# Values in an attention block: high and low half in one stationary tile, summed in DRAM

## The chip, the cores and the metric

The kernel runs on one core of one Trainium2 chip. The metric is device microseconds of one execution on that core, taken as the median of several runs of the same program. Times inside a run come from one profiled execution, as microseconds from its first instruction. PE is the matmul engine (PEld its weight load), DVE the vector engine, ACT the scalar engine, POOL is GpSimd, and SP issues most DMAs.

## The reference

One decoder block for S = 1024 positions and a model width of 1024, in float32. The part that matters here, cut down:

```
proj = rmsnorm(x) @ w_in + b_in
u_pool, q, k, v, gates = split(proj)          # 512, 512, 128, 128, 2048 columns
# pooling: four groups of 128 channels, windows 2, 4, 8, 16
y_pool = ((window_mean(u) - u) @ w_pool) * pool_scale
# attention: 8 query heads of 64, 2 key/value heads, blocks of 128 queries, window 128
p = softmax([s * 0.125 + mask, sink])[..., :-1]
o = einsum('bnhgqk,bnkhd->bnqhgd', p, v)      # y_attn
merged = sigmoid(g_pool) * (y_pool @ w_branch_pool) + sigmoid(g_attn) * (y_attn @ w_branch_attn)
x = x + rmsnorm(merged @ w_out)
x = x + rmsnorm(relu(rmsnorm(x) @ w_up)**2 @ w_down)
```

## The kernel before

**Halves.** Every float32 operand of a matmul is split into a high float32r part (a cast, `split` L99, by ACT) and a low part (the value minus the high part, L104, by DVE). A product is then three matmuls: high by high, low by high, high by low. All matmuls accumulate in PSUM banks of 128x512.

**Stages.** The program goes through the projections (to about 81 us), the attention loop (81 to 182), the gate products (to 334), the attention and pooling branches with their merge (334 to about 420), the output projection and the MLP. In the first two stages the order of work on PE, DVE and ACT is the order of the code. POOL's and SP's orders, and all orders in the branch stage, are set by the framework's scheduler.

**The attention loop** (L767 to L810) has one turn n for each of the eight blocks of 128 queries. A turn transposes the probabilities of block n (`attend_t`, L376; two head groups kv, one bank "at" each, split by ACT and DVE into four tiles), issues the scores of block n+2 (`score`, L333), forms the masked copy of the probabilities (`attend_own`, L385), transposes q and k of block n+3 into two "at" banks and splits them (`post_qkv`, L294; tiles `qt`, `khi`, `klo`), runs softmax pieces (maximum on DVE, L349 to L351; exponentials on ACT, L357 and L359; the scale on DVE, L363 to L365), and ends with the product of probabilities and values (`attend_v`, L394). Three banks carry the name "at", three "mm". Between these pieces `fill(t)` takes about t microseconds of PE work from a generator `others()`: the projections of the remaining blocks, then for each pooling group `u_half` (L575, u of one half of the positions) and `wb_half` (L594, the pooling weights folded into the branch weights). Half way through each `u_half` the list `between[th]` is flushed: weight splits and copies for later (casts `wh` and L561 on ACT, low halves L104 and L562 on DVE).

**The value product.** `attend_v(n)` for n > 0 has two terms: all probabilities by the values of block n−1, and the masked ones by the difference of the values of blocks n and n−1 (`dv`). A stationary tile holds, for high and low, the columns [head 0, zeros, head 1]: a slice of 128 columns from 0 or from 64 puts one head into its own half of the output rows and zeros into the other. So both head groups accumulate in one bank, with 3 × 2 matmuls a term. POOL makes these tiles (`split_v`, L281 writes the zeros). Two ACT copies of 128x256 (L398) move the bank into `y` tiles, which live in SBUF until four blocks are done and are then stored to DRAM in four transfers of 512 KB.

**Pooling sums.** `pool_in` (L655 to L665) adds the bias and builds windowed sums by doubling steps on DVE: one step for window 2, four for window 16. For groups 2 and 3 `pump` runs single steps inside turns 4 to 7 of the loop, before u goes to DRAM. For groups 0 and 1 the raw u goes to DRAM, and `pool_part` sums it in the branch stage.

**The branch stage.** Eight attention branches (`branch`, L422 and L424 on PE) each fill two banks "mm" of four and end with two gate products on DVE (L918). `pool_part` follows branches 2, 3, 5 and 6: it loads one group of u (L923, tile `d`), sums it where needed, and splits it. `load_attn` brings `y` back from DRAM ahead of the stage.

Of the kernel before, what the change touches and what calls it, by code (L numbers as in the profile page):

```python
# [8 lines left out]
F32 = mybir.dt.float32  # L9
F32R = mybir.dt.float32r  # L10
# [4 lines left out]
P = 128  # L15
# [33 lines left out]

@with_exitstack  # L50
def block_kernel(ctx: ExitStack, tc, xt, x, consts, vecs, sinks, b_qkv, g_post, g_mlp, g_mlp_post,
                 w_qkv, w_u, w_g, w_pool, w_bp, w_ba, w_o, w_up, w_dn, x1_dram, spill, wbp_dram, f_dram, out):
    nc = tc.nc
    act, dve, pool, pe = nc.scalar, nc.vector, nc.gpsimd, nc.tensor

# [9 lines left out]
    z_dram, y_dram, u_dram = (spill[i:j] for i, j in ((0, 16), (16, 20), (20, 24)))  # L65
    cnt = [0]

    def nm(s):
        cnt[0] += 1
        return f"{s}_{cnt[0]}"  # L70
# [25 lines left out]
    def f32(ap):  # L96
        return ap.bitcast(F32)
# [150 lines left out]
    khi = at("khi", 1, [S], F32R)  # L248
    klo = at("klo", 1, [S], F32R)
    vs, dvs = {}, {}  # L250
    y = [[None, None], [None, None]]
    for th in range(2):
        for kh in range(2):
            y[th][kh] = yy.tile([P, 2, 512], F32, tag="y", name=nm("y"))
    qts = {}

    tfs = {}

    def pre_qkv(n):
        tf = y[1][n - 2].rearrange("p a b -> p (a b)") if n in (2, 3) else at("qkv", 3, [1024])  # L260
# [126 lines left out]

    def attend_v(n):
        pt, pc = probs.pop(n)
        yb = bank("at", [4, P])  # L390
        mms = [(v, p, kv, j) for v, p in (((vs[n - 1], pt), (dvs[n], pc)) if n else ((vs[0], pt),))
               for j in ((0, 0), (1, 0), (0, 1)) for kv in range(2)]
        for j, (v, p, kv, (vh, ph)) in enumerate(mms):
            pe.matmul(yb.rearrange("p m q -> p (m q)"), v[:, vh, kv * HD:kv * HD + P],  # L394
                      p[ph][:, 4 * kv:4 * kv + 4].rearrange("p i q -> p (i q)"), start=j == 0, stop=j == len(mms) - 1)
        c = (n % 4) * P
        for g in range(2):
            act.copy(y[n // 4][g][:, :, c:c + P], yb[:, 2 * g:2 * g + 2])  # L398


    rb = bcp.tile([P, 1024], F32, tag="bc", name="rb_all")
# [163 lines left out]
    def u_half(gi, th):  # L565

        if th == 0:
            ut[gi] = ga_.tile([P, S], F32, tag="ga", name=nm("u"))
        (whi, wlo), u = wu[gi], ut[gi]
        sl = slice(th * 512, (th + 1) * 512)  # L570
        b = bank("mm")

        mms = [(k, xh, 0) for k in range(NK) for xh in range(2)] + [(k, 0, 1) for k in range(NK)]
        for j, (k, xh, h) in enumerate(mms):
            pe.matmul(b, (whi, wlo)[h][:, k, :], xr(k, xh, th), start=j == 0, stop=j == len(mms) - 1)  # L575
            if j == 7:
# [4 lines left out]
        if th == 1 and gi < 2:  # L581
            nc.sync.dma_start(u_dram[gi], u)
        elif th == 1:
            us[gi] = u

    def wb_half(gi, dj):

# [13 lines left out]
                                  t.rearrange("c (m n) -> c m n", n=P))  # L601
        between[dj].append(out)

    us, ut, wt, wpts = {}, {}, {}, []

    def others():
        for n in range(4, NT):
# [114 lines left out]
    with tc.manual_schedule(engines={mybir.EngineType.PE, mybir.EngineType.DVE, mybir.EngineType.Activation}):  # L722
        for n in range(NT):
            fill(0.34)
            pe.matmul(bss[:, n:n + 1], sq[:, n * P:(n + 1) * P], ones, start=n == 0, stop=n == NT - 1)
        rsqrt(r1, bss[:, :NT], NT)
        act.activation(warm, r1[:, :1], AF.Exp)
        pre_qkv(0)
        pre_qkv(1)
        fill(5.4)  # L730
        post_qkv(0)
        pre_qkv(2)
        fill(2.8)
# [24 lines left out]
        sums = {}  # L758

        def pump(k, gi):  # L760

            if gi not in sums:
                sums[gi] = pool_in(gi, us[gi], y_place)
            for _ in range(k):
                next(sums[gi])

        for n in range(NT):  # L767
            attend_t(n)
            if n == 0:
                softmax_exp(1, LOW)  # L770
            if n + 2 < NT:
                score(n + 2, 0)
            if n + 1 < NT:
                softmax_exp(n + 1, HIGH)
            if n + 2 < NT:
                score_prev(n + 2, 0)
            attend_own(n)
# [16 lines left out]
            if n == 4:  # L794
                pump(1, 3)
            elif n == 5:
                pump(2, 3)
                nc.sync.dma_start(u_dram[3], us.pop(3))
            elif n == 6:
                pump(2, 2)  # L800
                load_x(0, lambda: at("qkv", 3, [S]))
            elif n == 7:
                pump(1, 2)
                nc.sync.dma_start(u_dram[2], us.pop(2))
                gt.prepare(0)
            fill(3.0 if n == NT - 1 else 4.2)
            attend_v(n)
            if n % 4 == 3:
                for kh in range(2):
# [73 lines left out]
    def load_attn():  # L883
        for kh in range(2):
            for th in range(2):
                ws = stage([2, 512])
                nc.sync.dma_start(flat(ws), y_dram[2 * th + kh])
# [565 lines left out]
```

## Time and profile before

| | us |
|---|---|
| runs, median (lowest to highest of 3) | 1137.67 (1136.68 to 1137.91) |
| span of the profiled execution | 1136.2 |
| ACT's copy of one value bank, 2 x 128x256 (L398), a pair | 0.65 |
| DVE's low half of a weight, 128x1024 (L104) | 1.22 |
| gate product in the branch stage (L918), a pair | 1.28 |
| PE busy, in the windows from 80 to 182 us | 102.00 of 102.00 |

The profiled execution is one run with the span from its first to its last instruction; a run's device time has about 1.5 us around that. In the rows of the timeline the first number is the start, the second the duration; a note in brackets tells how long the engine stood still before, and which engine ended that. In the rows of groups the mean of one instruction is in nanoseconds.

### The profile page before, as it was taken

The numbers are of one execution on the slowest core, as the hardware profiler recorded it, in microseconds if no ns is written. First come the engines' busy times: TensorE is split into PE (matmuls) and PEld (weight loads), VectorE is DVE, ScalarE is ACT, GpSimd is POOL, SyncE is SP. The second block draws the span as 40 slices with busy tenths as digits, with TensorE's granted clock in tenths as the row PEclk, the third lists the DMA queues.
The fourth block names the chain that finished last, engine by engine and source line by source line (L and its number), as shares of the span: only waits on it lengthen the run. The fifth ranks groups of instructions, "written<-read, shape, count | busy, mean of one in ns | idle before, by whom it ended". The sixth has DMA issues, their size and how long they took to land.

```text
span 1136.2 us, 14006 instructions
## 1 busy us (share of the span) xinstructions
PE 1120.7 (99%) x5213; PEld 926.6 (82%) x5213; DVE 822.7 (72%) x1210; ACT 523.9 (46%) x912; POOL 65.3 (6%) x110
## 2 busy tenths in 40 slices
PE   8999999999999999999999999999999999999997
PEld 7888888888888888888788888888888888888885
DVE  7668797899956685677998666666457955446887
ACT  6346655454522234455655444444444345344352
POOL 3432100000000230000000000000000000000000
PEclk9999999999999999999999999999999999999999
DMA  7202338356664434333265343434687765332652
GB/s 247 84 1 74 116 108 297 129 188 229 217 234 161 139 142 155 112 145 111 108 236 206 139 164 142 160 146 156 223 321 278 244 198 193 109 93 74 219 191 91
DMA packets 72052, 186.94 MB, mean 165 GB/s; under 512 B 6448, under 2 KB 10672, under 8 KB 71984
## 3 DMA queue, kind: packets, MB, share of 16 engines
q1 hardware_dynamic: 66368, 166.38, 42.0%
q10 hardware_dynamic: 5616, 19.66, 4.5%
q8 instruction: 41, 0.67, 0.2%
q14 instruction: 27, 0.22, 0.1%
HBM read 132.54 MB, written 53.48 MB: 164 GB/s over the span
## 4 chain that ended last, share of the span: by engine, by line
PE 91%; DVE 5%; ACT 2%; DMA 2%; issue 1%; DVEq 0%
PE mm L485 22%; PE at L485 15%; PE at L1291 14%; PE mm L1291 11%; PE mm L1008 6%; PE mm L422 5%; PE mm L575 4%; PE mm L183 3%; PE mm L424 3%; PE at L394 2%; PE sc L333 1%; PE at L1008 1%; PE at L192 1%; DVE wh L104 1%; DMA st<-in_w_up_dram 1%
## 5 line engine op out<-in xcount | busy, mean ns | idle before, releaser
L1291 PE MATMUL at<-ar,wh 128*128 128x512 f32 x744 | 169.6, 389 | 0.0
L1291 PEld LDWEIGHTS at<-ar,wh 128*128 128x128 f32 x744 | 139.6, 188 | 29.3 <-DVE ar L104 0.4
L1291 PE MATMUL mm<-ar,wh 128*128 128x512 f32 x576 | 131.0, 389 | 0.0
L104 DVE TENSOR_TENSOR wh<-raw,wh 128x1024 fp32r<-128x1024 f32 x53 | 64.8, 1223 | 85.4 <-ACT wh L101 85.4
L1291 PEld LDWEIGHTS mm<-ar,wh 128*128 128x128 f32 x576 | 108.1, 188 | 22.5
L101 ACT CAST wh<-raw 128x1024 fp32r<-128x1024 f32 x53 | 55.8, 1053 | 135.8 <-PE at L1291 61.9
L101 ACT CAST wh<-st 128x512 fp32r<-128x512 f32 (+1 forms) x105 | 66.2, 642 | 104.0 <-PE at L485 31.0
L104 DVE TENSOR_TENSOR wh<-st,wh 128x512 fp32r<-128x512 f32 (+1 forms) x105 | 81.8, 790 | 25.9 <-ACT wh L101 23.3
L485 PE MATMUL mm<-gr,wh 128*128 128x512 f32 x309 | 74.5, 390 | 0.1
L485 PEld LDWEIGHTS mm<-gr,wh 128*128 128x128 f32 x309 | 57.7, 188 | 12.3 <-ACT g L1073 0.5
L485 PE MATMUL mm<-T,wx 128*128 128x512 f32 x288 | 67.6, 389 | 0.0
L485 PEld LDWEIGHTS mm<-T,wx 128*128 128x128 f32 x288 | 54.1, 188 | 11.2
L485 PE MATMUL at<-T,wx 128*128 128x512 f32 x252 | 59.1, 389 | 0.0
L485 PEld LDWEIGHTS at<-T,wx 128*128 128x128 f32 x252 | 47.3, 188 | 9.8
L485 PE MATMUL mm<-x,wh 128*128 128x512 f32 x240 | 55.2, 389 | 0.0
L485 PEld LDWEIGHTS mm<-x,wh 128*128 128x128 f32 x240 | 45.0, 188 | 9.4
L104 DVE TENSOR_TENSOR ar<-B,ar 128x1024 fp32r<-128x1024 f32 x37 | 45.1, 1219 | 5.3 <-ACT ar L101 5.0
L575 PE MATMUL mm<-x,wh 128*128 128x512 f32 x192 | 47.5, 396 | 0.0
L485 PE MATMUL at<-gr,wh 128*128 128x512 f32 x174 | 42.4, 390 | 0.0
L101 ACT CAST ar<-B 128x1024 fp32r<-128x1024 f32 x37 | 38.9, 1050 | 7.5 <-DMA B<-in_w_dn_dram 4.7
L575 PEld LDWEIGHTS mm<-x,wh 128*128 128x128 f32 x192 | 35.2, 188 | 7.7
L485 PEld LDWEIGHTS at<-gr,wh 128*128 128x128 f32 x174 | 32.6, 188 | 7.3 <-DVE gr L104 0.5
(368 smaller groups left out, 2182.9 us busy)
## 6 DMA issues: line engine op xcount, KB each, us to landing
raw<-f_dram SPq DMA_DIRECT2D x53, 512.0 KB, 3.7
f_dram<-g SPq DMA_DIRECT2D x30, 512.0 KB, 3.3
B<-in_w_dn_dram SPq DMA_DIRECT2D x24, 512.0 KB, 6.2
st<-in_w_up_dram SPq DMA_DIRECT2D x22, 512.0 KB, 3.5
st<-in_w_g_dram SPq DMA_DIRECT2D x18, 512.0 KB, 3.6
f_dram<-g ACTq DMA_DIRECT2D x17, 512.0 KB, 2.6
g<-spill_dram SPq DMA_DIRECT2D x16, 512.0 KB, 4.5
raw<-in_w_dn_dram SPq DMA_DIRECT2D x16, 512.0 KB, 4.6
```

The costliest lines, as they stand in the source:

```text
L101: act.copy(hi, src)
L104: eng.tensor_tensor(lo, src, f32(hi), ALU.subtract)
L183: pe.matmul(bq, xs_[k][n // 4][:, xh, n % 4 * P:(n % 4 + 1) * P], wq[k][:, h, :], start=k == 0 and j == 0, stop=k == NK - 1 and j == 2)
L192: pe.matmul(bkv_of(n), xs_[k][n // 4][:, xh, n % 4 * P:(n % 4 + 1) * P], wkv[k // 2][:, h, k % 2, :], start=k == 0 and j == 0 and not (joi ...
L333: pe.matmul(sb[:, kv, i, :nk], qt[r, qx, m * P:(m + 1) * P], kx[r, k0:k0 + nk], start=j == 0, stop=j == 2)
L394: pe.matmul(yb.rearrange("p m q -> p (m q)"), v[:, vh, kv * HD:kv * HD + P], p[ph][:, 4 * kv:4 * kv + 4].rearrange("p i q -> p (i q)"), st ...
L422: pe.matmul(bs[th], whi[:, k, :], rhs(k, hl, th), start=k == 0 and hl == 0, stop=False)
L424: pe.matmul(bs[th], wlo[:, k, :], rhs(k, 0, th), start=False, stop=k == nk - 1)
L485: pe.matmul(b, w[:, wh, kt, :], xo[kt][:, xh, :], start=not after and kt == 0 and j == 0, stop=kt == 3 and j == 2, skip_group_check=after)
L575: pe.matmul(b, (whi, wlo)[h][:, k, :], xr(k, xh, th), start=j == 0, stop=j == len(mms) - 1)
L1008: pe.matmul(obs[n][dj], l, wos[k][whl][:, dj * 512:(dj + 1) * 512], start=k == 0 and hl == 0 and whl == 0, stop=k == NK - 1 and hl == 1)
L1291: pe.matmul(bs[t], fo[fh][:, k2, t * P:(t + 1) * P], wo_[wh][:, k2, :], start=not after and s2 == 0 and k2 == 0 and j == 0, stop=s2 == NS ...
```

## The change

- **One stationary tile for both halves.** `split_v` now makes tiles with the columns [high, low] of one head, without zeros. One matmul with the high part of p then gives high by high in output rows 0 to 63 and low by high in rows 64 to 127; a second one, with the low part of p, adds the rest. A term needs two matmuls for each head group. Each head group has its own bank, and the loop's `bank("at")` is called twice.
- **The halves are added in DRAM.** ACT copies each bank whole into a tile `yt` (a fresh one for each turn, from a pool of four). SP writes rows 0 to 63 into `y_dram`, in two transfers of 128 KB; POOL then adds rows 64 to 127 in two accumulating transfers of the same size. `y_dram` has a new layout, and `load_attn` reads it so.
- **Held flushes.** While the `fill` right ahead of `attend_v` runs, `u_half` does not flush `between[th]`; that is done after `attend_v`.
- **Later pooling sums.** `pump` is gone. All four groups store their raw u, and `pool_part` sums each.

The core of the diff:

```
     def split_v(src, tag, bufs):
-        t = at(tag, bufs, [2, 3, HD], F32R)
-        pool.memset(f32(t[:, :, 1, :]), 0.0)
-        split(t[:, 0, ::2, :], t[:, 1, ::2, :], src, pool, pool)
-        return t.rearrange("p l a d -> p l (a d)")
+        t = at(tag, bufs, [2, 2, HD], F32R)
+        split(t[:, :, 0, :], t[:, :, 1, :], src, pool, pool)
+        return t.rearrange("p a l d -> p a (l d)")
...
     def attend_v(n):
         pt, pc = probs.pop(n)
-        yb = bank("at", [4, P])
-        mms = [(v, p, kv, j) for v, p in (((vs[n - 1], pt), (dvs[n], pc)) if n else ((vs[0], pt),))
-               for j in ((0, 0), (1, 0), (0, 1)) for kv in range(2)]
-        for j, (v, p, kv, (vh, ph)) in enumerate(mms):
-            pe.matmul(yb.rearrange("p m q -> p (m q)"), v[:, vh, kv * HD:kv * HD + P],
-                      p[ph][:, 4 * kv:4 * kv + 4].rearrange("p i q -> p (i q)"), start=j == 0, stop=j == len(mms) - 1)
-        c = (n % 4) * P
-        for g in range(2):
-            act.copy(y[n // 4][g][:, :, c:c + P], yb[:, 2 * g:2 * g + 2])
+        yt = yy.tile([P, 2, 4, P], F32, tag="y", name=nm("yt"))
+        terms = ((vs[n - 1], pt), (dvs[n], pc)) if n else ((vs[0], pt),)
+        rows = y_dram[n // 4][:, :, n % 4 * P:(n % 4 + 1) * P]
+        for kv in range(2):
+            yb = bank("at", [4, P])
+            mms = [(v, p) for v, pp in terms for p in pp]
+            for j, (v, p) in enumerate(mms):
+                pe.matmul(flat(yb), v[:, kv, :], flat(p[:, 4 * kv:4 * kv + 4]), start=j == 0, stop=j == len(mms) - 1)
+            act.copy(yt[:, kv], yb)
+        for kv in range(2):
+            nc.sync.dma_start(rows[kv * HD:(kv + 1) * HD], yt[:HD, kv])
+        for kv in range(2):
+            pool.dma_start(rows[kv * HD:(kv + 1) * HD], yt[HD:, kv], accum_op=ALU.add)
...
     # u_half
             if j == 7:
-                flush(between[th])
+                if held[0]:
+                    held.append(th)
+                else:
+                    flush(between[th])
...
     # the loop
-            if n in (4, 5):
-                pump(1, 3)
-            elif n == 6:
-                pump(1, 2)
             fill(3.6)
...
+            held[0] = True
             fill(3.0 if n == NT - 1 else 4.2)
             attend_v(n)
-            if n % 4 == 3:
-                for kh in range(2):
-                    nc.sync.dma_start(y_dram[n // 4 * 2 + kh], flat(y[n // 4][kh]))
+            held[0] = False
+            while len(held) > 1:
+                flush(between[held.pop()])
...
     def pool_part(gi):
         u = yy.tile([P, S], F32, tag="y", name=nm("d"))
         nc.sync.dma_start(u, u_dram[gi])
-        if gi < 2:
-            for _ in pool_in(gi, u, y_place):
-                pass
+        for _ in pool_in(gi, u, y_place):
+            pass
```

Three places in the order of the engines. On PE, at the end of turn 3 (`s_190` to `s_197` are the split probabilities, `at_1444` the value bank, `at_1463` and `at_1470` the banks of the transposes of turn 4), before:

```order
L594 MATMUL mm_1440<-wh_1133,wpt 128x512
L394 MATMUL at_1444<-s_190_1301,v_741 128x512 x4
L394 MATMUL at_1444<-s_191_1302,v_741 128x512 x2
L394 MATMUL at_1444<-s_196_1337,dv_915 128x512 [waits DVE_49]
L394 MATMUL at_1444<-s_196_1337,dv_915 128x512 x3
L394 MATMUL at_1444<-s_197_1338,dv_915 128x512 [waits DVE_49]
L394 MATMUL at_1444<-s_197_1338,dv_915 128x512
L376 MATMUL at_1463<-cst,s_171_1167 128x128 [waits DVE_49]
L376 MATMUL at_1463<-cst,s_171_1167 128x128 x3
L376 MATMUL at_1470<-cst,s_171_1167 128x128 [waits DVE_49]
L376 MATMUL at_1470<-cst,s_171_1167 128x128 x3
```

The same place now (`at_1439` and `at_1445` are the two value banks, `at_1457` and `at_1464` those of the transposes):

```order
L392 MATMUL at_1439<-s_194_1296,v_736 128x512
L392 MATMUL at_1439<-s_195_1297,v_736 128x512
L392 MATMUL at_1439<-s_200_1332,dv_907 128x512 [waits DVE_49]
L392 MATMUL at_1439<-s_201_1333,dv_907 128x512 [waits DVE_49]
L392 MATMUL at_1445<-s_194_1296,v_736 128x512 [waits DVE_49]
L392 MATMUL at_1445<-s_195_1297,v_736 128x512
L392 MATMUL at_1445<-s_200_1332,dv_907 128x512
L392 MATMUL at_1445<-s_201_1333,dv_907 128x512
L371 MATMUL at_1457<-cst,s_173_1162 128x128 [waits DVE_49]
L371 MATMUL at_1457<-cst,s_173_1162 128x128 x3
L371 MATMUL at_1464<-cst,s_173_1162 128x128 [waits Activation_49]
L371 MATMUL at_1464<-cst,s_173_1162 128x128 x3
```

The wait for DVE that stood at the first transposes (the bank that held the transposed q, until DVE has its low half) stands at the second value bank, and the second group of transposes waits for ACT, for the copy of the first value bank.

On ACT, at the end of turn 2 (`es` and `s_171` or `s_173` are the exponentials, `wh` a weight of the filler work, `s_190` or `s_194` the probabilities of turn 3), before:

```order
L357 ACTIVATE es_1226<-es_1226 128x8
L359 ACTIVATE s_171_1167,den_1227<-s_171_1167,nmx_1225 128x128 x4
L101 CAST wh_1270<-st_1118 128x1024
L398 COPY y_459<-at_1286 128x2x128
L398 COPY y_460<-at_1286 128x2x128
L101 CAST s_190_1301<-at_1303 128x512
L101 CAST s_190_1301<-at_1310 128x512
```

And now:

```order
L352 ACTIVATE es_1221<-es_1221 128x8
L354 ACTIVATE s_173_1162,den_1222<-s_173_1162,nmx_1220 128x128 x4
L393 COPY yt_1275<-at_1276 128x512
L393 COPY yt_1275<-at_1282 128x512
L101 CAST wh_1292<-st_1111 128x1024
L101 CAST s_194_1296<-at_1298 128x512
L101 CAST s_194_1296<-at_1305 128x512
```

The weight's cast has gone behind the value copies, and stands right ahead of the casts of the next turn's probabilities.

On DVE, in the branch stage around the gate products of branches 3 to 5 (`g` the gate, `mm` the bank, `d` and `t` the pooling sums), before:

```order
L104 TENSOR_TENSOR yplo_3412<-d_3409,yphi_3411 128x1024
L104 TENSOR_TENSOR yplo_3454<-d_3451,yphi_3453 128x1024
L918 TENSOR_TENSOR g_3288<-g_3288,mm_3296 128x512
L918 TENSOR_TENSOR g_3288<-g_3288,mm_3297 128x512
L104 TENSOR_TENSOR wh_3420<-st_3417,wh_3419 128x512
L918 TENSOR_TENSOR g_3337<-g_3337,mm_3345 128x512
L918 TENSOR_TENSOR g_3337<-g_3337,mm_3346 128x512
```

And now:

```order
L898 TENSOR_TENSOR g_3256<-g_3256,mm_3264 128x512
L898 TENSOR_TENSOR g_3256<-g_3256,mm_3265 128x512
L660 COPY t_3386<-t_3383 128x4
L663 SCALAR_TENSOR_TENSOR d_3377<-t_3386,d_3377 128x1017
L664 TENSOR_TENSOR t_3386<-t_3386,cst 128x7
L104 TENSOR_TENSOR wh_3401<-st_3398,wh_3400 128x512
L665 TENSOR_TENSOR d_3377<-t_3386,d_3377 128x7
L659 TENSOR_TENSOR t_3435<-d_3432 128x1023
L104 TENSOR_TENSOR yplo_3393<-d_3377,yphi_3392 128x1024
L898 TENSOR_TENSOR g_3305<-g_3305,mm_3313 128x512
L898 TENSOR_TENSOR g_3305<-g_3305,mm_3314 128x512
```

The sums of groups 2 and 3 stand between the gate products; the first step of the last group (`d_3432`) stands ahead of branch 4's.

More of the change, by code (lines that the diff above doesn't have):

```diff
@@ L51, in block_kernel @@
 def block_kernel(ctx: ExitStack, tc, xt, x, consts, vecs, sinks, b_qkv, g_post, g_mlp, g_mlp_post,
-                 w_qkv, w_u, w_g, w_pool, w_bp, w_ba, w_o, w_up, w_dn, x1_dram, spill, wbp_dram, f_dram, out):
+                 w_qkv, w_u, w_g, w_pool, w_bp, w_ba, w_o, w_up, w_dn, x1_dram, spill, y_dram, wbp_dram, f_dram, out):
     nc = tc.nc
@@ L63, in block_kernel @@
     psum = {"pool": psa_pool.__enter__(), "bufs": {"sc": 1, "at": 3, "mm": 3}}
-    z_dram, y_dram, u_dram = (spill[i:j] for i, j in ((0, 16), (16, 20), (20, 24)))
+    z_dram, u_dram = (spill[i:j] for i, j in ((0, 16), (16, 20)))
     cnt = [0]
@@ L250, in block_kernel @@
     vs, dvs = {}, {}
-    y = [[None, None], [None, None]]
-    for th in range(2):
-        for kh in range(2):
-            y[th][kh] = yy.tile([P, 2, 512], F32, tag="y", name=nm("y"))
     qts = {}
@@ L259, in pre_qkv @@
     def pre_qkv(n):
-        tf = y[1][n - 2].rearrange("p a b -> p (a b)") if n in (2, 3) else at("qkv", 3, [1024])
+        tf = yy.tile([P, 1024], F32, tag="y", name=nm("y")) if n in (2, 3) else at("qkv", 3, [1024])
         tfs[n] = tf
@@ L580, in u_half @@
         dve.tensor_tensor(u[:, sl], b, rb[:, sl], ALU.mult)
-        if th == 1 and gi < 2:
+        if th == 1:
             nc.sync.dma_start(u_dram[gi], u)
-        elif th == 1:
-            us[gi] = u
     def wb_half(gi, dj):
@@ L602, in wb_half @@
         between[dj].append(out)
-    us, ut, wt, wpts = {}, {}, {}, []
+    ut, wt, wpts, held = {}, {}, [], [False]
     def others():
@@ L757, in block_kernel @@
         fill(3.7)
[L758 to L765, printed above, removed]
         for n in range(NT):
@@ L793, in block_kernel @@
                 softmax_exp(n + 2, LOW)
[L794 to L800, printed above, removed]
+            if n == 6:
                 load_x(0, lambda: at("qkv", 3, [S]))
             elif n == 7:
-                pump(1, 2)
-                nc.sync.dma_start(u_dram[2], us.pop(2))
                 gt.prepare(0)
+            held[0] = True
             fill(3.0 if n == NT - 1 else 4.2)
             attend_v(n)
-            if n % 4 == 3:
-                for kh in range(2):
-                    nc.sync.dma_start(y_dram[n // 4 * 2 + kh], flat(y[n // 4][kh]))
+            held[0] = False
+            while len(held) > 1:
+                flush(between[held.pop()])
         gt.prepare(1)
@@ L886, in load_attn @@
                 ws = stage([2, 512])
-                nc.sync.dma_start(flat(ws), y_dram[2 * th + kh])
+                nc.sync.dma_start(ws, y_dram[th][:, 2 * kh:2 * kh + 2])
                 hi = xp.tile([P, 2, 512], F32R, tag="x", name=nm("yahi"))
@@ L1444 @@
     x1 = nc.dram_tensor("x1_dram", (NT, P, D), F32, kind="Internal").ap()
-    spill = nc.dram_tensor("spill_dram", (24, P, S), F32, kind="Internal").ap()
+    spill = nc.dram_tensor("spill_dram", (20, P, S), F32, kind="Internal").ap()
+    yd = nc.dram_tensor("y_dram", (2, P, 4, 512), F32, kind="Internal").ap()
     wbp = nc.dram_tensor("wbp_dram", (8, P, 4, P), F32, kind="Internal").ap()
@@ L1449 @@
     with tile.TileContext(nc) as tc:
-        block_kernel(tc, *args, x1, spill, wbp, fd, out)
+        block_kernel(tc, *args, x1, spill, yd, wbp, fd, out)
     r = run_bass_kernel_spmd(nc, [arrays], core_ids=[0])
```

## The prediction

> **What bounds the kernel now.** I read the busy times on the page and the chain that ended last first, then the busy time by windows around the two places that the change touches: the attention loop (87 to 182 us) and the branch stage (from 334 us).
>
> ```profile
> span 1136.2 us, 14006 instructions
> PE 1120.7 (99%) x5213; PEld 926.6 (82%) x5213; DVE 822.7 (72%) x1210; ACT 523.9 (46%) x912; POOL 65.3 (6%) x110
> ...
> PE 91%; DVE 5%; ACT 2%; DMA 2%; issue 1%; DVEq 0%
> ```
>
> PE is busy for 99% of the span and is 91% of the chain. The windows (stretch, sum, then PE, PEld, DVE, ACT, POOL with their counts, granted clock, DMA share, GB/s) show the same in the stages concerned:
>
> ```profile
> 80.00:100.00 20.00, 20.00 (x144) 17.45 (x143) 16.14 (x28) 11.23 (x41) 1.95 (x6) 1.00 0.08 27
> 100.00:120.00 20.00, 20.00 (x122) 16.28 (x121) 15.94 (x23) 13.10 (x43) 8.88 (x19) 1.00 0.31 106
> 120.00:140.00 20.00, 20.00 (x120) 16.14 (x119) 16.92 (x26) 13.07 (x39) 2.26 (x7) 1.00 0.38 128
> 140.00:160.00 20.00, 20.00 (x112) 16.27 (x111) 19.04 (x32) 10.65 (x37) 2.01 (x6) 1.00 0.17 57
> 340.00:360.00 20.00, 20.00 (x90) 16.57 (x89) 15.26 (x24) 7.09 (x9) 0.00 (x0) 1.00 0.68 230
> 360.00:380.00 20.00, 20.00 (x90) 16.57 (x89) 7.69 (x13) 3.44 (x5) 0.00 (x0) 1.00 0.18 56
> ```
>
> PE has no gap in any of them, at full clock: a matmul that goes shortens the span, as long as nothing that PE needs comes late instead. The follower is DVE: 19.04 of 20 us in the late loop, 7.69 of 20 at 360. So work taken from DVE in the loop is relief, and work put at 360 has room.
>
> **The matmuls that go.** These are the value product's matmuls, and its place in the third full turn of the loop (n=3):
>
> ```profile
> L394 PE MATMUL at<-s,v x48: 389/389/393, 87.1 to 178.8; 128*128 128x512 f32 x48
> L394 PE MATMUL at<-s,dv x42: 389/389/393, 100.9 to 180.2; 128*128 128x512 f32 x42
> ```
> ```profile
> 128.19 1.52 PE L394 MATMUL at<-s,v 128*128 128x512 f32 x6
> 129.55 1.53 PE L394 MATMUL at<-s,dv 128*128 128x512 f32 x6
> 130.91 1.03 PE L376 MATMUL at<-cst,s 128*128 128x128 f32 x8
> ```
>
> Twelve matmuls take 130.91 − 128.19 = 2.72 us, so one costs 0.227 us (389 ns is its latency; they are pipelined). Of 48 + 42 = 90, n=0 keeps 4 of 6 and the other seven turns 8 of 12: 60 stay, 30 go. 30 × 0.227 = **6.8 us**: 0.45 in n=0 and 0.91 in each later turn. The new matmuls have the same shape, so I give them the same 0.227.
>
> **The waits that come.** Two things now stand close behind one another. First, the second value bank of a turn is the one that the q transposes of post_qkv(n+3) just used, so its first matmul waits for DVE's low half of q. Before, that wait lay 2.72 us behind the start of the value matmuls, at the transposes; now 0.91 us. Second, the second head group's transposes of attend_t(n+1) wait until ACT has copied the first value bank. ACT in n=2 and n=3, and DVE between:
>
> ```profile
> 112.47 0.21 ACT L357 ACTIVATE es<-es 128x8 f32<-128x8 f32 x1 [2.14 <-DVE es L351]
> ...
> 114.13 1.03 ACT L101 CAST wh<-st 128x1024 fp32r<-128x1024 f32 x1
> 117.00 0.65 ACT L398 COPY y<-at 128x256 f32<-128x256 f32 x2 [1.84 <-PE at L394]
> 117.53 1.10 ACT L101 CAST s<-at 128x512 fp32r<-128x512 f32 x2
> ...
> 128.08 0.21 ACT L357 ACTIVATE es<-es 128x8 f32<-128x8 f32 x1 [3.41 <-DVE es L351]
> ...
> 129.65 0.19 ACT L359 ACTIVATION_READ_ACCUMULATOR s<-s,nmx 128x1 f32 x1
> ```
> ```profile
> 99.03 0.68 DVE L104 TENSOR_TENSOR qt<-at,qt 128x512 fp32r<-128x512 f32 x1
> ...
> 112.36 0.68 DVE L104 TENSOR_TENSOR qt<-at,qt 128x512 fp32r<-128x512 f32 x1
> ...
> 115.19 1.22 DVE L104 TENSOR_TENSOR wh<-st,wh 128x1024 fp32r<-128x1024 f32 x1 [1.36 <-ACT wh L101]
> 118.17 1.29 DVE L104 TENSOR_TENSOR s<-at,s 128x512 fp32r<-128x512 f32 x2 [1.75 <-ACT s L101]
> ...
> 127.96 0.69 DVE L104 TENSOR_TENSOR qt<-at,qt 128x512 fp32r<-128x512 f32 x1
> ```
> ```profile
> 99.51 1.52 PE L394 MATMUL at<-s,v 128*128 128x512 f32 x6
> ...
> 114.07 1.52 PE L394 MATMUL at<-s,v 128*128 128x512 f32 x6
> ```
> ```profile
> L335 ACT COPY s<-sc 128x512 f32<-128x512 f32 x11 | 6.5, 588 | 8.6 <-PE sc L333 8.3
> ```
>
> *Turn n=2.* With 0.45 + 0.91 won, its value matmuls start at 112.7. The copies now have the shape of L335, 0.59 us. The first bank is full 0.91 later, at 113.6; the exponentials (1.78 us from es at 112.47, by n=3's 129.84 − 128.08 = 1.76) end at 114.2 if they don't come earlier, so the copy ends at 114.8. PE would want the bank after eight matmuls and four transposes, 1.82 + 0.5 after the start, at 115.0. I take **0.2** us.
>
> *Turn n=3* is the dearest. The held flush puts the cast of wh (1.03) and DVE's low half of it (1.22) behind both copies: copies to about 115.3, cast to 116.3, low half to 117.5. DVE begins its two splits of s then, against 118.17 before: 0.67 us earlier. From there to the low half of q, DVE has no pause in the trace, so that ends at 128.65 − 0.67 = 128.0. PE has won 0.45 + 0.91 + 0.91 − 0.2 = 2.1 by then: value matmuls from 126.1, second bank wanted at 127.0. It waits 1.0. The exponentials also come 0.67 earlier, ending at 129.2, the first copy at 129.8; PE would be at the second transposes 1.4 after 128.0, at 129.4: 0.4 more. **1.4 us** in this turn.
>
> *Turn n=4* has no held weight in front of it (the copies are followed by the casts of s directly), so DVE follows PE closer; I take half, **0.7**. *Turn n=5* has no q transposes left, only the copy behind the exponentials; DVE loses a pooling sum ahead of them. I take **0.3**. Turns 6 and 7 have no exponentials. At n=1 the low half of q ends at 99.71, and the second bank is wanted at 99.51 − 0.45 + 0.91 = 99.97; at n=2 the two are 113.04 and 113.6: room, though little at n=1.
>
> Sum: 0.2 + 1.4 + 0.7 + 0.3 = **2.6 us** come back as waits; both ends for the range are 0 (all inside the slack) and 6.8 (four turns at n=3's price, 5.6, and more behind).
>
> **What moves beside PE.** The longer copies add 2 × 0.48 − 0.65 = 0.3 us a turn to ACT (11 to 13 of 20 busy), counted above. The memsets leave POOL. Pooling sums leave the loop:
>
> ```profile
> L659 DVE TENSOR_TENSOR t<-t 128x1022 f32<-128x1022 f32 (+2 forms) x5 | 6.1, 1213 | 0.0
> ...
> L659 DVE TENSOR_TENSOR t<-u 128x1023 f32<-128x1023 f32 x2 | 2.4, 1217 | 0.0
> L663 DVE SCALAR_TENSOR_TENSOR u<-t,u 128x1009 f32<-128x1009 f32 (+1 forms) x2 | 2.4, 1210 | 0.0
> L655 ACT ACTIVATE u<-u,vec 128x1024 f32<-128x1024 f32 x2 | 2.3, 1150 | 0.0
> ```
>
> That is 6.1 + 2.4 + 2.4 = 10.9 us on DVE, some 12 with the short pieces. They turn up between the gate products of the branch stage:
>
> ```profile
> 361.65 1.29 DVE L918 TENSOR_TENSOR g<-g,mm 128x512 f32<-128x512 f32 x2 [3.55 <-PE mm L424]
> ```
> ```profile
> 334.47 0.39 PE L422 MATMUL mm<-yahi,wh 128*128 128x512 f32 x1
> ...
> 339.91 0.39 PE L422 MATMUL mm<-yahi,wh 128*128 128x512 f32 x1
> ```
> ```profile
> DMA to landing us min/median/max: 4.3/6.3/7.6
> ```
>
> A branch takes PE 339.91 − 334.47 = 5.44 us; with four banks, two a branch, the gate product of branch m must be done when branch m+2 starts, at 334.47 + 5.44 (m+2): 5.44 us of room. DVE idles 3.55 us a branch from 361 on. Twelve us over four branches is 3 each: it fits, barely. The two loads of u stand ahead: DVE's first sum of the last group waits for a load that can only start when a buffer is free, by my count at about 358 in the old clock. Landing in 4.5 us, plus 1.15 (L655), 1.2 (L659) and 0.7 for the first half of the gate product, ends at 365.6; branch 6 wants that bank at 367.1. Landing in 6.3 costs 0.3; in 7.6 it costs 1.6 there, and about 2 with the next branches. At 360 to 380 the DMA share is 0.18 against 0.68 before, so I take the short landing, **0**.
>
> **The DMAs.** Four stores of 512 KB become sixteen of 128 KB on SP and sixteen that add, on POOL. No accumulating transfer is in the trace. The nearest rows of issue, SP's, are 0.33 us each, and a turn has two. What stands behind them on POOL is the split of the next V:
>
> ```profile
> 145.99 0.46 POOL L104 TENSOR_TENSOR dv<-df,dv 128x128 fp32r<-128x128 f32 x1
> ...
> 177.67 1.52 PE L394 MATMUL at<-s,v 128*128 128x512 f32 x6
> ```
>
> The last V is ready at 146.5 and used at 179: over 30 us to spare. From the first store at about 91 to 177 POOL has 86 us, less the 15 that it is busy in the four windows from 80 to 160: 71 us for the eight transfers ahead of the last V, so PE stalls only from about 9 us each. Bounds: 0, and all that lies above that; I take 0, by the 0.33.
>
> **Sum.** 6.8 − 2.6 = 4.2 us off the profiled 1136.2: 1132.0. The runs' median is 1137.67, 1.5 above that span, so **1133.5**.
>
> **The rivals.**
> *All of it arrives:* DVE, relieved of its sums, and the exponentials come earlier by as much as PE. For it: DVE idles in the early loop (15.94 of 20). Against: the 10 us without a pause before 127.96. The time is 1137.7 − 6.8 = 1130.9. Chance 0.17.
>
> *The loop closes on itself:* each of turns 1 to 4 waits as n=3 does, 4 × 1.4, and n=5 adds 0.3: 5.9 of 6.8 are gone, 1136.8; with the loads landing in 7.6 us, 1138.8. Here belongs, too, that the change doesn't shorten PE at all. For it: PE's turn is 14.1 − 0.9 = 13.2 us, and the round from the second bank over copy, cast, DVE's low half and the 10.5 us to q is 0.9 + 0.6 + 1.0 + 1.2 + 10.5 = 14.2. Against: only one turn has a full wh held. Chance 0.22.
>
> *Slower:* the last pooling sums sit ahead of the gate products on DVE, and each branch from m=4 on waits for loads. It decides against the change when the wait passes 4.2 + 2.3 = 6.5 us, which by the sum above needs a landing of 6.0 + 6.5 = 12.5 us; at 15.2, twice the worst row, the wait is 9.2 and the time 1142.7. Against: the three landings quoted. Chance 0.06.
>
> *Slower by POOL:* if an accumulating transfer holds POOL for 12 us, eight cost 96, 25 more than the 71 us: 1158. DVE is busy 19.04 of 20 us at 140, so a transfer that POOL could issue only while DVE rests would take 20 times 0.33, 6.6 us: short of the 9. Chance 0.04. The Trainium skill ("DMA: Bandwidth & Descriptors", section SWDGE vs HWDGE vs iDMA) states such a lock: transfers that accumulate come from GpSimd alone, and the descriptor rings that it writes for them lie in the SBUF state that a two-port mode of DVE keeps it out of. No run here shows it; by that rule an issue would stretch towards the 6.6.
>
> **How the numbers follow.** 4.2 less, give or take 1.2: chance 0.51, all of it faster by more than 0.2% (2.3 us), about the least that a measurement of this kernel tells from no change. With the full gain, 0.17: faster 0.68; of the closed loop nearly all is within 0.2%: same 0.21; slower 0.11. The range goes from 1130.5 (the full gain) to 1138.5 (the closed loop with late loads).
>
> **What would show it.** L392's matmuls should be 60 at 0.227 us. PE should show waits at L392's second bank on DVE (qt), longest at n=3, and at L371 on ACT (yt), in sum 1 to 4 us. DVE's busy time falls in 140 to 182 and rises in 350 to 380. If PE waits at L422 for DVE's L898, the loads were late; if at L392 for POOL, the transfers. A loop that is shorter by 6.8 us makes me wrong in the waits, a PE gap after 182 in the rest.

## The result, and the profile after

| | before | after |
|---|---|---|
| runs, median (lowest to highest of 5) | 1137.91 (1136.68 to 1139.01) | 1133.95 (1132.40 to 1134.51) |
| ratio of after to before, 95% interval | | 0.9963 (0.9951 to 0.9975) |
| span of the profiled execution | 1136.2 | 1132.7 |
| first value matmul of n=0 to the end of the last of n=7 | 93.30 | 89.03 |

The change makes the kernel faster, by 4.0 us in the medians; forecast were 4.2, with 1133.5. (A run's device time lies 1.7 to 1.8 us above its own span, 1134.51 and 1132.7 here; the 1.5 given ahead is the median of the runs before less the span of one of them.) The page of after, its first lines and its chain:

```profile
span 1132.7 us, 14023 instructions
PE 1114.8 (98%) x5183; PEld 920.9 (81%) x5183; DVE 820.6 (72%) x1210; ACT 526.7 (47%) x912; POOL 77.8 (7%) x111
...
PE 87%; DVE 7%; ACT 3%; DMA 2%; issue 1%; SPq 0%; DVEq 0%; ACTq 0%
```

PE has 30 instructions less (5213 to 5183) and is busy 5.9 us less, yet the span fell by 3.5 only, and DVE and ACT have taken shares of the chain. The windows of after (stretch, sum, busy time of PE, PEld, DVE, ACT, POOL, clock, DMA share, GB/s) show where:

```profile
120.00:140.00 20.00, 19.01 (x114) 14.86 (x113) 17.88 (x25) 11.26 (x32) 4.95 (x8) 1.00 0.74 168
140.00:160.00 20.00, 19.26 (x107) 15.39 (x107) 12.88 (x22) 13.19 (x41) 3.48 (x6) 1.00 0.49 113
160.00:180.00 20.00, 20.00 (x94) 16.63 (x93) 13.77 (x19) 10.37 (x25) 4.04 (x4) 1.00 0.81 198
360.00:380.00 20.00, 20.00 (x90) 16.58 (x89) 15.13 (x26) 4.52 (x8) 0.00 (x0) 1.00 0.26 79
```

PE has gaps now in two windows of the loop, 1.0 and 0.7 us, and none at 360 to 380, where DVE went from 7.69 to 15.13 us busy. The gaps in PE's timeline of after (start, duration; in brackets the pause ahead and who ended it):

```profile
126.51 0.62 PE L392 MATMUL at<-s,v 128*128 128x512 f32 x2
126.96 0.61 PE L392 MATMUL at<-s,dv 128*128 128x512 f32 x2
128.54 0.73 PE L392 MATMUL at<-s,v 128*128 128x512 f32 x2 [0.97 <-DVE qt L104]
129.12 0.62 PE L392 MATMUL at<-s,dv 128*128 128x512 f32 x2
129.57 1.28 PE L371 MATMUL at<-cst,s 128*128 128x128 f32 x8
...
148.75 0.39 PE L328 MATMUL sc<-klo,qt 64*128 64x256 f32 x2 [0.16 <-DVE s L337]
...
155.95 0.60 PE L371 MATMUL at<-cst,s 128*128 128x128 f32 x4
157.12 0.66 PE L371 MATMUL at<-cst,s 128*128 128x128 f32 x4 [0.57 <-ACT yt L393]
```

At n=3 the second bank would have started four matmuls after the first, at 127.42; it starts 1.12 late, and DVE's low half of q ends that wait. At n=5 the second transposes come 0.7 late, behind ACT's copy of the first bank. (A bracket counts from the modelled end of the last matmul, so it shows a little less than the start times do.)

Counted by turns, from the first value matmul of one to that of the next:

| turn | before | forecast without waits | after | waits |
|---|---|---|---|---|
| 0 to 1 | 12.42 | 11.97 | 11.98 | 0.0 |
| 1 to 2 | 14.56 | 13.65 | 13.65 | 0.0 |
| 2 to 3 | 14.12 | 13.21 | 13.21 | 0.0 |
| 3 to 4 | 14.34 | 13.43 | 14.89 | 1.46 |
| 4 to 5 | 13.40 | 12.49 | 12.73 | 0.24 |
| 5 to 6 | 11.55 | 10.64 | 11.45 | 0.81 |
| 6 to 7 and the last product | 12.91 | 11.10 | 11.12 | 0.0 |

The waits are 2.5 us in all, and 93.30 − 6.8 + 2.5 = 89.0. The first value matmul itself starts 0.58 later (87.09 and 87.67), and what follows the last one takes 956.0 against 955.8: −4.27 + 0.58 + 0.2 = −3.5, the difference of the spans. The 0.58 arises in the first stage: behind a pause of PE at 53 us the matmuls resume at 55.52 in before and 56.17 in after, and at 55.18 to 55.90 in the other traces, most of which have the same order up to there. So it is taken as scatter, not as an effect of the change.

### The profile page after: what moved, and what is told of

It is laid out like the page before. It is cut to its first block, busy times and chain, and to the rows that moved or that the text cites. A ratio compares the mean times of both kernels' runs of the same rounds, so it can differ in the third digit from the quotient of the medians.

```text
span 1132.7 us, 14023 instructions
## 1 busy us (share of the span) xinstructions
PE 1114.8 (98%) x5183; PEld 920.9 (81%) x5183; DVE 820.6 (72%) x1210; ACT 526.7 (47%) x912; POOL 77.8 (7%) x111
## 4 chain that ended last, share of the span: by engine, by line
PE 87%; DVE 7%; ACT 3%; DMA 2%; issue 1%; SPq 0%; DVEq 0%; ACTq 0%
PE mm L484 22%; PE at L484 16%; PE at L1270 14%; PE mm L1270 12%; PE mm L987 6%; PE mm L421 5%; PE mm L183 3%; PE mm L423 3%; PE mm L574 2%; PE at L987 1%; PE at L192 1%; DVE wh L104 1%; PE at L392 1%; PE sc L328 1%; DMA st<-in_w_up_dram 1%
## 5 line engine op out<-in xcount | busy, mean ns | idle before, releaser
L104 DVE TENSOR_TENSOR wh<-raw,wh 128x1024 fp32r<-128x1024 f32 x53 | 64.8, 1223 | 83.4 <-ACT wh L101 83.4
L104 DVE TENSOR_TENSOR wh<-st,wh 128x512 fp32r<-128x512 f32 (+1 forms) x105 | 81.8, 789 | 29.6 <-ACT wh L101 27.1
L104 DVE TENSOR_TENSOR ar<-B,ar 128x1024 fp32r<-128x1024 f32 x37 | 45.1, 1219 | 6.6 <-ACT ar L101 6.4
```

What stands on the lines that cost most here:

```text
L104: eng.tensor_tensor(lo, src, f32(hi), ALU.subtract)
```

## The experiments

"Stretch" is the time from the first value matmul to the end of the last (the start of PE's next row), from one trace. It doesn't hold the scatter of the first stage, and so tells differences of some 0.1 us where the medians need 1 to 2: it is the same within 0.03 in after, e6, e7 and e8. The ratio is to the kernel before as it ran alongside.

| run | stretch | median | ratio to before, 95% interval |
|---|---|---|---|
| before | 93.30 | 1137.91 | |
| after | 89.03 | 1133.95 | 0.9963 (0.9951 to 0.9975) |
| e1_flush_first | 88.95 | 1132.89 | 0.9965 (0.9952 to 0.9979) |
| e2_q_first | 90.74 | 1136.17 | 0.9993 (0.9984 to 1.0002) |
| e3_exp_next_turn | 87.86 | 1132.94 | 0.9960 (0.9947 to 0.9974) |
| e4_both | 86.70 | 1131.39 | 0.9950 (0.9938 to 0.9963) |
| e5_sums_in_loop | 97.10 | 1145.87 | 1.0073 (1.0058 to 1.0088) |
| e6_no_sums | 89.03 | 1132.12 | 0.9954 (0.9938 to 0.9971) |
| e7_plain_store | 89.06 | 1133.62 | 0.9967 (0.9954 to 0.9980) |
| e8_ring (one run) | 89.04 | 1131.97 | |
| e9_both_no_hold | 88.09 | 1132.89 | 0.9961 (0.9949 to 0.9974) |
| e10_sums_ring | 91.41 | 1141.59 | 1.0036 (1.0023 to 1.0049) |
| e11_sums_own | 90.58 | 1139.34 | 1.0019 (1.0009 to 1.0030) |
| e12_moves_on_before | 93.30 | 1137.21 | 0.9997 (0.9987 to 1.0007) |

### Where do the 2.5 us wait? e2, e3 and e4

DVE makes the low half of q behind the maximum; ACT copies the value banks behind exponentials. Each was moved alone, then both.

e2_q_first:

```
                 score_prev(n + 2, 1)
-                softmax_max(n + 2)
             if n + 3 < NT:
                 post_qkv(n + 3)
+            if n + 2 < NT:
+                softmax_max(n + 2)
```

> The changed kernel, with post_qkv(n+3) in front of softmax_max(n+2) in the code, so that DVE makes the low half of q before the maximum. Theory: PE's wait for q at the second value bank of n=3 (1.1 us) is gone, but the exponentials come 0.96 us later (0.68 + 0.28 of DVE work goes in front of them), so the copy of the first value bank ends later, and the transposes at n=2 and n=3 wait for ACT about 0.8 and 2.3 us: net about 2 us longer than the changed kernel, 1136. Rival (q is the only wait that counts): 1.1 us shorter, 1132.8.

The stretch grew by 1.71 (2 were expected). In PE's timeline of e2 the wait for q at n=3 is gone, and a longer one for the copy has come:

```profile
131.20 0.66 PE L371 MATMUL at<-cst,s 128*128 128x128 f32 x4 [1.99 <-ACT yt L393]
```

The second bank follows 0.45 behind the first bank's last pair (127.25 and 127.70); then the second transposes stand for 2 us until ACT is through with its exponentials.

e3_exp_next_turn:

```
-            if n == 0:
-                softmax_exp(1, LOW)
             if n + 2 < NT:
                 score(n + 2, 0)
             if n + 1 < NT:
-                softmax_exp(n + 1, HIGH)
+                softmax_exp(n + 1, range(8))
...
-            if n + 2 < NT:
-                softmax_exp(n + 2, LOW)
```

> The changed kernel, with the first four exponentials of a block moved behind the next turn's attend_t, beside the other four: the value copies have nothing in front of them on ACT but the casts of q. Theory: the waits for the copy at attend_t (0.25 at n=3, 0.24 at n=4, 0.7 at n=5) are gone; the 1.1 us for q at n=3 stays, since DVE's chain is the same: 1.0 us shorter than the changed kernel, 1133.0. Rival (the loop's length over ACT and DVE is what binds): the exponentials only shift the wait to the scale of the probabilities, no gain.

The stretch fell by 1.17 (1.0 expected): no wait for ACT is left, and the one for q at n=3 stays, with 0.94 in its bracket.

e4_both has both diffs.

> Both moves together: q's low half ahead of the maximum, and all exponentials in the next turn. Theory: all waits between 80 and 182 us go, so 2.3 us shorter than the changed kernel, 1131.6, span about 1130.4, PE busy 20.00 of 20 in each window. Rival (the loop over copy, cast of wh, DVE's low half and the s splits is too long by itself): a wait of about 1 us stays at n=3 or n=4 in another place, 1132.8.

The stretch fell by 2.33, to 86.70, against 86.50 with no waits at all; the median is 1131.39, where 1131.6 was expected. The windows of e4:

```profile
120.00:140.00 20.00, 20.00 (x121) 16.38 (x120) 18.92 (x30) 11.97 (x37) 4.96 (x8) 1.00 0.73 161
140.00:160.00 20.00, 19.84 (x111) 16.16 (x110) 14.07 (x19) 14.35 (x48) 4.49 (x7) 1.00 0.63 146
```

Only the 0.2 us at n=4 is left, a score matmul that waits for DVE (L337). So 2.3 of the 2.5 us that came back are these two waits. To move the exponentials alone returned their own share, 1.17. To move q alone put the exponentials later and lost more than it won; with the exponentials out of the way, the same move is worth 1.16 (87.86 to 86.70). e4_both is the fastest version of the study, 5.7 us below the kernel before in its own comparison (1137.11).

e12_moves_on_before puts the same two diffs on the kernel before.

> The kernel before, with the two moves of e4_both alone (q's low half ahead of the maximum, all exponentials in the next turn). Theory (the 2.3 us that e4_both wins over the changed kernel are waits that the change brought, and PE has no wait in the loop before): the stretch from the first to the last value matmul stays at 93.3 us within 0.2, the median at the kernel before's, ratio 1.000. Rival (the moves are worth something by themselves): 1 to 2 us shorter, ratio 0.998 to 0.999.

Stretch 93.30 and ratio 0.9997: the moves are worth nothing where the waits aren't.

### Does holding the flush pay? e1 and e9

```
-            held[0] = True
             fill(3.0 if n == NT - 1 else 4.2)
```

> The changed kernel, but the flush of weights is no longer held: it comes inside the fill again, ahead of the value product. Theory (the returned 2.5 us are waits for DVE's low half of q at the second value bank, 1.1 us at n=3, and for ACT's copy of the first value bank behind exponentials, 0.25, 0.24 and 0.7 us at n=3, 4, 5): the cast of wh now stands ahead of the copies at n=2 and n=5 and L560 ahead of them at n=4, so the transposes of attend_t wait there about 0.8, 1.7 and 0.6 us, while DVE gets to the splits of n=3 about 0.5 us earlier and the wait for q at n=3 goes. Net about 1.4 us longer than the changed kernel, 1135.3. Rival (the held weight is itself what lengthens the loop): the wait at n=3 goes and nothing comes in its place, 1.1 us shorter, 1132.8.

Neither came: the stretch is 88.95, the same as after's. The wait at n=3 did go (13.43 for that turn), the one at n=4 grew from 0.24 to 0.58 and the one at n=5 fell from 0.81 to 0.39; but turn 1 got longer by 1.48, where the theory had seen nothing. ACT and PE in e1:

```profile
101.66 0.62 ACT L101 CAST wpt<-st 128x512 fp32r<-128x512 f32 x1
102.18 1.14 ACT L560 ACTIVATE wh<-st,vec 128x1024 fp32r<-128x1024 f32 x1
103.23 1.05 ACT L393 COPY yt<-at 128x512 f32<-128x512 f32 x2
```
```profile
103.85 0.66 PE L371 MATMUL at<-cst,s 128*128 128x128 f32 x4 [1.28 <-ACT yt L393]
```

The flush of turn 1 holds two weights, 1.6 us of ACT behind the exponentials, and the copy comes after both. The wait at n=3 didn't go because DVE came earlier, as the theory had it: the low half of q ends 40.75 us behind the first value matmul, in after 40.81. PE comes to it 1.45 us later, by what it lost in turn 1. So holding moves a wait of 1.5 us from turn 1 to turn 3; by itself it gains nothing measurable here.

e9_both_no_hold is e4_both with the same line taken out.

> e4_both, with the flush of weights no longer held. Theory (holding pays only because the value copies wait behind what stands in front of them on ACT; with the exponentials gone the weight's cast runs in ACT's idle time, ahead of the value matmuls' end): the stretch from the first to the last value matmul stays at e4_both's 86.7 us within 0.4, the median near 1131.4. Rival (holding is needed by itself, to keep the casts off the copies): 1 us or more longer, by waits at attend_t's transposes.

The rival came: 88.09, 1.39 more than e4_both; turn 1 is 1.58 longer and turn 4 0.19 shorter. The cast of wpt began only at 100.48, after the value matmuls had begun at 98.87, so ACT's idle time ahead of them was of no use. ACT, then PE:

```profile
100.48 0.62 ACT L101 CAST wpt<-st 128x512 fp32r<-128x512 f32 x1 [4.71 <-DVE qkv L261]
```
```profile
102.68 0.66 PE L371 MATMUL at<-cst,s 128*128 128x128 f32 x4 [1.39 <-ACT yt L393]
```

What ended ACT's idle time is DVE's last use of the bias in `pre_qkv` (L261): by the code, wpt takes the buffer of that bias. With the exponentials out of the way, holding is worth 1.4 us here; whether it still would be with a buffer free for wpt wasn't tried.

### Are the stores and the moved sums free? e6, e7 and e8

e6_no_sums leaves the sums of groups 2 and 3 out of `pool_part` (`if gi < 2:` stands ahead of them again, and nothing else).

> The changed kernel, without any sums for groups 2 and 3: their raw u goes on as it is, which leaves out the pooling of those two groups. Theory: in the branch stage the sums lie beside the matmuls, so the stretch from 320 to 420 us and the median (about 1134) stay as in the changed kernel, within 0.3 us of the stretch. Rival (the sums or their loads hold gate products back): 1 to 3 us shorter.

The stretch is 89.03 and PE is busy for all of 320 to 420, as in after: from PE's side the 12 us of sums in the branch stage cost nothing, and what follows the stretch takes 956.0 in both. (The median is 1.8 lower, but the intervals of the two ratios overlap.) The reason is in after's rows:

```profile
357.92 1.16 ACT L655 ACTIVATE d<-d,vec 128x1024 f32<-128x1024 f32 x1 [5.06 <-DMA d<-spill_dram]
```
```profile
361.38 1.28 DVE L898 TENSOR_TENSOR g<-g,mm 128x512 f32<-128x512 f32 x2
```
```profile
363.37 0.39 PE L421 MATMUL mm<-yahi,wh 128*128 128x512 f32 x1
```

The last load was issued at 354.4 and had landed by 357.9, 3.5 us later. DVE's gate product of branch 4 starts at 361.4 and has freed the first bank at about 362.0; branch 6 wants it at 363.4, so 1.4 us were left.

e7_plain_store: `nc.sync.dma_start(...)` in place of `pool.dma_start(..., accum_op=ALU.add)`, which leaves out the addition of the halves.

> The changed kernel, with the second half of each bank stored by a plain DMA of SP over the first, not added by POOL: this leaves out the addition of the halves. Theory: the accumulating transfers lie beside the matmuls and cost nothing, so the stretch from the first to the last value matmul stays at 89.0 us within 0.3, and so does what follows. Rival (their traffic or POOL's pauses delay the loads of weights and the splits of V): 0.5 us or more shorter.

Stretch 89.06, the same turn by turn within 0.04: the accumulating transfers cost the loop's matmuls nothing. What follows takes 955.4, 0.6 less than in after; the other traces without the sums in the loop have 955.6 to 956.5, so that is hardly more than scatter.

e8_ring: `dynamic_dma_scratch_size=4096` for 1024, one run.

> The changed kernel, with four times the scratch memory for the descriptors of POOL's transfers (4096 for 1024). In the trace POOL pauses 2.6 to 5 us between the two accumulating transfers of a turn, with nothing shown that it waits for. Theory (no room for the second's descriptors until the first has been done): the second follows the first at once, about 1.0 us after its start; the span stays as it is, since POOL has time. Rival (the second waits for the first's landing for another reason): the pause stays.

The theory came. POOL's rows in after, then in e8:

```profile
91.98 1.18 POOL L397 DMA_DIRECT2D y_dram<-yt  x1 [2.35 <-DMA y_dram<-yt]
95.71 1.02 POOL L397 DMA_DIRECT2D y_dram<-yt  x1 [2.56 <-issue]
```
```profile
89.74 2.22 POOL L397 DMA_DIRECT2D y_dram<-yt  x2 [2.34 <-DMA y_dram<-yt]
```

All eight pairs of e8 leave together. The turns have the lengths of after's within 0.05 from turn 1 on; time on POOL is free here.

### Why had the sums to go? e5, e10 and e11

e5_sums_in_loop brings `pump`, its calls and `if gi < 2:` back as they were before.

> The changed kernel with one part undone: the sums of groups 2 and 3 are back in turns 4 to 7 of the attention loop, at the places they had before. Theory (the value copies wait behind the exponentials, and these follow DVE's maximum): a step of 1.37 us ahead of the maximum in turns 4 and 5 makes the exponentials later by as much, so the transposes of attend_t wait about 0.4 us more after turn 4 and 1.4 more after turn 5. The stretch from the first to the last value matmul is 1.8 us longer than the changed kernel's 89.0, the median about 1135.7. Rival (DVE has 7 of 20 us idle there now, so the sums fit): no difference.

Both were wrong: 8.1 us more in the stretch and 1145.87 for the median, slower than before the change. 1.5 are turns 4 and 5, near the 1.8 expected. The rest begins in turn 6 on ACT, then on PE:

```profile
172.05 1.07 ACT L393 COPY yt<-at 128x512 f32<-128x512 f32 x2 [8.51 <-DMA y_dram<-yt]
```
```profile
172.69 1.11 PE L371 MATMUL at<-cst,s 128*128 128x128 f32 x4 [3.68 <-ACT yt L393]
```

Of the 6.6 us of turn 6, 3.9 are PE's pause; the other 2.7 go to slower matmuls behind it. The granted clock (third number from the end) is 0.66 in that window; from 174 to 176 us it is 0.50:

```profile
170.00:180.00 10.00, 7.31 (x23) 5.94 (x24) 5.45 (x9) 5.19 (x9) 1.00 (x1) 0.66 0.59 105
```

The copy waits for an accumulating transfer: the sums' tiles and the `yt` share four buffers, so with sums in between a buffer comes round sooner, and it is free only when POOL's slow pair has landed. Two runs test that.

e10_sums_ring is e5 with `dynamic_dma_scratch_size=4096`.

> e5_sums_in_loop (sums of groups 2 and 3 back in turns 4 to 7), with 4096 for 1024 of descriptor memory, so that the two accumulating transfers of a turn leave POOL together. Theory (most of e5's 12 us is ACT's 8.5 us at the value copy of turn 6, which waits for a buffer that the sums and the copies share until an accumulating transfer has landed, and POOL's pauses make that transfer late; 1.5 us is the maximum's delay by DVE's sums): the wait of 8.5 us falls to 1 us or less, the median to about 1136. Rival (DVE has no time for the sums): it stays near 1145.

The wait did nearly go (turn 6 takes 10.16 for 15.86, the stretch 91.41), but the median is 1141.59, 5.6 above the 1136 expected. e11_sums_own leaves the scratch at 1024 and gives the sums other buffers:

```
-                sums[gi] = pool_in(gi, us[gi], y_place)
+                sums[gi] = pool_in(gi, us[gi], lambda: at("qkv", 3, [1024]))
```

> e5_sums_in_loop, with the sums' intermediate tiles in the three buffers of the projections (tag qkv) rather than in the four that the value copies use. Theory (the shared buffers are the cause): ACT's wait for an accumulating transfer at the value copies is gone, the 1.5 us by DVE's sums ahead of the maximum stay; the stretch from the first to the last value matmul is 90.5 us, the median about 1135.5. Rival (DVE's load): near 1145 as e5.

The stretch is 90.58, as expected, and the median 1139.34, 3.8 above. What the stretch doesn't hold comes 15 us behind it. PE in e11, SP in e11, and SP in after:

```profile
191.59 8.67 PE L484 MATMUL mm<-x,wh 128*128 128x512 f32 x31 [2.91 <-ACT wh L101]
```
```profile
176.80 0.92 SPq L806 DMA_DIRECT2D spill_dram<-u  x1
177.81 0.52 SPq L395 DMA_DIRECT2D y_dram<-yt  x1
...
183.14 2.07 SPq L448 DMA_DIRECT2D st<-in_w_g_dram  x2
```
```profile
176.34 0.33 SPq L448 DMA_DIRECT2D st<-in_w_g_dram  x1
176.76 1.53 SPq L395 DMA_DIRECT2D y_dram<-yt  x2
```

With the sums in the loop, the load of a gate weight stands behind the stores of u and of yt on SP and goes out at 183.1, not 176.3. Its cast waits 4.2 us for the landing, and PE 2.9 us for the cast. That the place on SP makes it late is read from these rows, not tested. Behind the pause the clock is at half again (e11):

```profile
192.00:194.00 2.00, 2.00 (x6) 1.47 (x6) 2.00 (x4) 1.06 (x3) 0.00 (x0) 0.50 1.09 376
```

The 144 matmuls that follow start over a time about 1.4 us longer than 144 × 0.227. So the sums in the loop would cost this change three things: 1.5 us by DVE's delay of the maximum (in e5 the exponentials of turn 5 come 1.5 later, counted from the first value matmul), up to 6.6 by the shared buffers, and 4 to 5 after the loop (1136.9 − 176.27 = 960.6 in e11, 956.0 in after), of which the pause and the slow matmuls behind it are 4.3.

## Why the prediction was right, point by point

- **Thirty matmuls at 0.227, 6.8 us.** Right: turns 0, 1, 2 and 6 are shorter by 0.44, 0.91, 0.91 and 0.88, and e4_both's stretch is 6.6 below before. The rows in after:

```profile
L392 PE MATMUL at<-s,v x32: 389/389/500, 87.7 to 176.0; 128*128 128x512 f32 x32
L392 PE MATMUL at<-s,dv x28: 388/389/393, 100.1 to 176.5; 128*128 128x512 f32 x28
```

- **Waits of 2.6 us.** 2.5 came. At n=3, 1.46 (forecast 1.4): 1.12 of it for q, where 1.0 stood, the rest behind the copy. The chain was the one named; these rows of DVE in after answer to those of before:

```profile
116.90 1.23 DVE L104 TENSOR_TENSOR wh<-st,wh 128x1024 fp32r<-128x1024 f32 x1 [2.32 <-ACT wh L101]
118.04 1.28 DVE L104 TENSOR_TENSOR s<-at,s 128x512 fp32r<-128x512 f32 x2
...
127.80 0.68 DVE L104 TENSOR_TENSOR qt<-at,qt 128x512 fp32r<-128x512 f32 x1
```

  The weight's low half stands right ahead of the splits of s, which begin at 118.04 as against 118.17, though PE reached its value matmuls 1.7 us earlier (126.51 and 128.19). Counted from the first value matmul, which is 0.58 later in after, DVE gained 0.71 (forecast 0.67) and PE 2.26. The other terms were mis-sized and cancelled, so the nearness of the sum is in part luck. At n=2, 0.2 was forecast and none came: by the prediction's own numbers the copy ended at 114.8 and PE wanted the bank at 115.0, which is 0.2 of room, not a wait. At n=4 it was 0.7 against 0.24, and at a score matmul, not at the banks. At n=5 it was 0.3, set without a sum, against 0.81. For n=5 the failing step is that a pooling sum less on DVE would bring the exponentials forward by more than PE gains. They came 1.88 us earlier (156.72 to 154.84), PE's value matmuls 1.80 (155.93 to 154.13), so the copy stayed behind. Before (ACT, PE), then ACT in after:

```profile
156.72 0.21 ACT L357 ACTIVATE es<-es 128x8 f32<-128x8 f32 x1 [4.57 <-DVE es L351]
```
```profile
155.93 1.52 PE L394 MATMUL at<-s,v 128*128 128x512 f32 x6
```
```profile
154.84 0.21 ACT L352 ACTIVATE es<-es 128x8 f32<-128x8 f32 x1 [4.49 <-DVE es L346]
...
156.50 1.04 ACT L393 COPY yt<-at 128x512 f32<-128x512 f32 x2
```

  A pair of the longer copies takes ACT 1.04 to 1.07, 0.4 more than before, where 0.3 was forecast.
- **The moved sums at nothing.** Right (e6), and the room at branch 6 was nearly as counted: 1.4 us, where 367.1 − 365.6 = 1.5 stood. That is luck in part: the load landed in 3.5 us, not 4.5, and DVE's low half of the group before (L104, 1.2) stood ahead of the gate product too, which the sum didn't have. What their move was worth wasn't seen: less by DVE's load in the loop than by the shared buffers, by the late gate weight, and by the clock behind both pauses (e5, e10, e11).
- **The transfers at nothing.** Right for the time (e7), wrong for the price: an accumulating transfer takes POOL 1.0 us, not 0.33, and its pair another 2.6 to 5 us of pause. The last V was still ready at 144.6, 31 us ahead of its use at 175.4.
- **The rivals.** The full gain is nearly what e4_both has: it needed both waits gone. The closed loop did not come: n=3 alone paid its price. The lock on POOL did not show: all sixteen issues took 1.00 to 1.18 us, with DVE at work (at 146.31 and 160.13) as at rest (165.72). No trace shows whether DVE was ever in the mode that the rule names.

## What to carry to other kernels

Where PE has no gaps, each matmul saved is worth its pitch, less what then comes late: list the waits that a shorter turn meets first, on each engine with what stands ahead of it in the queue, and see what a move puts later: the move of q lost 1.7 us alone and won 1.2 beside the other. A store that waits for a slow queue keeps its buffer: who shares the buffers decides whether the slow queue is free. And a pause of PE can cost more than its length, by the clock behind it.

## What the hardware showed that was not expected

**The accumulating transfers.** One of 128 KB in 512-byte pieces takes POOL 1.0 us and lands 3.3 to 8.4 us after issue (median 3.9). With 1024 of descriptor scratch the second of a pair waits until the first is done or nearly so; with 4096 it follows at once (e8).

**A short pause can halve the clock.** Ahead of the loop PE pauses 2.68 us at about 53 us in every trace. The windows right behind it (the third number from the end is the granted clock), in before and in e3:

```profile
56.00:58.00 2.00, 2.00 (x7) 1.57 (x6) 0.91 (x2) 0.00 (x0) 2.00 (x7) 0.52 0.00 0
58.00:60.00 2.00, 2.00 (x6) 1.30 (x5) 0.00 (x0) 0.00 (x0) 1.92 (x6) 0.62 0.00 0
```
```profile
56.00:58.00 2.00, 2.00 (x10) 1.67 (x9) 1.05 (x2) 0.00 (x0) 1.92 (x6) 1.00 0.00 0
58.00:60.00 2.00, 2.00 (x18) 1.45 (x18) 0.00 (x0) 0.47 (x1) 1.92 (x6) 1.00 0.00 0
```

The same twelve matmuls take 4.60 us there and 3.01 here. The pause is the same, the outcome isn't: e3, e8 and e11 kept the full clock, the other traces didn't. The first value matmul starts between 85.4 and 88.7 us in kernels whose order on PE up to there is the same: 85.4 to 85.7 with the clock kept, 88.2 and 88.7 (e1, e10) where the twelve took 5.49. That is a large part of the scatter of the spans (e3's 1129.1 among them), and why the stretch was used. The Trainium skill ("TensorE: Matmul & The Clock Gate", Part 1) has the clock fall to half after an idle window of about 3.4 us and asks for no gaps above that; here a gap of 2.68 us was enough in most traces. Later pauses agree: behind 2.04 us (e5, at 198.7), 2.91 (e11), 3.24 (e10) and 3.68 (e5) the clock read 0.50, behind 1.78 to 1.99 (e2, e5, e10, e11) it stayed at 1.00. What decides between the two at 2.68 wasn't tried.
